# Fifteen of the twenty weight-row sums in each feed-forward chunk issued on GpSimd in place of VectorE

## The chip, the cores and the metric

The kernel runs on one core of one Trainium2 chip. The metric is the device time of one execution in microseconds (us). The kernel before takes 1955.56 us, the median of three runs (1954.87 to 1957.17). The engines carry the names of the profile: PE (TensorE matrix products), PEld (its weight loads), DVE (VectorE), ACT (ScalarE), POOL (GpSimd) and SP (the engine that only issues DMAs here). Each engine takes its instructions strictly in program order and waits on semaphores for the others.

## The reference, cut to what matters

One layer of a hybrid model on 128 context tokens and 256 latent tokens, width 2048, everything in float32. The change lies in the last sub-layer:

```python
h = rmsnorm(x, lw['norm_pre_ffn']) * (1.0 + sc2) + sh2
ff = (jax.nn.silu(h @ lw['w_ffn_gate']) * (h @ lw['w_ffn_up'])) @ lw['w_ffn_down']
x = x + ga2 * rmsnorm(ff, lw['norm_post_ffn'])
```

The hidden width is 5632, and the 384 tokens are three blocks of 128.

## The kernel before, in words

**Split numbers.** Every matrix product is made with each float32 operand split in two parts: `hi`, the operand rounded to the matrix engine's format, and `lo`, the rest. A product is then three products (hi by hi, hi by lo, lo by hi). For each weight block of 128 partitions by 1024 elements (512 KB) ACT makes `whi` by a copy with rounding (line 1430), and DVE makes `wlo`, the block less `whi` (line 1441). Both stand in rings of four tiles.

**Chunks.** The hidden width is cut into 11 chunks of 512 columns. Chunk 0 is made in the plain way. For chunks 1 to 10 the kernel saves products by a scheme in the manner of Strassen's: it replaces some weight blocks by sums and differences of blocks. For the gate and up weights, with g0, g1, u0, u1 the upper and lower row halves of the chunk's gate and up blocks (each in four pieces, i = 0 to 3), the steps are

- A: products with u0; then u0's tile becomes g0 - u0 (`sum1`, line 1413, four sums)
- B: products with g0 - u0
- C: products with g1; the tile of g0 - u0 becomes g1 - g0 + u0 (`x`, line 1437, four sums) and g0's tile becomes g1 - g0 (`y`, line 1438, four sums)
- E: products with g1 - g0 + u0, which the C just ahead of it made
- F: products with g1 - g0
- G: products with u1; the tile of E becomes u1 less what stood there (line 1440, four sums)
- H: products with that last sum

A part of the down weights goes the same way in steps DA to DH, one piece each: one sum at DA (line 1443), two at DC (lines 1437 and 1438), one at DG (line 1440). That makes 12 + 8 = 20 sums in a chunk: 4 + 4 + 4 + 4 for gate and up, 1 + 1 + 1 + 1 for down. The down steps of a chunk run inside the following chunk, so chunks 1 to 9 hold 20 sums each, and chunk 10 only the 16 of gate and up. (Written out: 40 + 9 at each of lines 1437, 1438 and 1440, 40 at line 1413 and 9 at line 1443, 196 in all.) The order of the steps is written out by hand in `steps`: A, B, then C and E in turn, F and G in turn, then H, with the down steps in between.

**Where the blocks live.** Pieces of kinds A and B (and DA, DB) are loaded into resident slots `u` and `dw`, which the sums overwrite. Pieces of kinds C, G, D, DC and DG stream through a ring of two tiles named `raw`. A `raw` tile may be loaded anew only when all its readers are done: the ACT copy, the DVE rest, and the sums that read it.

**The order of work around a step.** Each step calls `grab2`: it takes the oldest finished pair (`whi`, `wlo`), lets SP issue loads into free tiles (`load_more`), and prepares a coming block (`split_next`): first the ACT copy, then up to three or four small waiting pieces of work from the list `pend`, then the sums of that block, then the rest `wlo`. The engines' own order is therefore the order of this text (a manual schedule). The list `pend` also holds `to_sums` (line 1634): ACT copies a product bank to an SBUF tile (line 1638) and POOL issues a DMA that adds it to a sum in DRAM (line 1642). Sixteen such DMAs are issued in a chunk from the second on, 128 in all, and before the change they are POOL's only work in chunks 1 to 10.

**Memory of the operands.** The sums and the rests read two operands that both lie in SBUF. The tiles `ptr`, `pgu`, `pdn`, `z`, `zx`, `prow` and `py` lie in PSUM, so a DVE instruction that reads one of them has at most one operand in SBUF. Before the change POOL makes elementwise sums at three places only: lines 1181 and 225 just ahead of the feed-forward sub-layer, and line 1856 at the very end.

Of the kernel before, what the change touches and what calls it, by code (L numbers as in the profile page):

```python
# [96 lines left out]
def tile_step(ctx: ExitStack, tc: tile.TileContext, a, o):  # L97
    nc = tc.nc
    PE, ACT, DVE, POOL, SP = nc.tensor, nc.scalar, nc.vector, nc.gpsimd, nc.sync
# [512 lines left out]
    with ExitStack() as s:  # L612
# [203 lines left out]
        for c in range(2):  # L816

            dst = a2.rearrange("p (h d j) -> p d h j", d=2, j=P)[:, c]
            raw, up = (x.rearrange("p (h j) -> p h j", j=P) for x in (raw3[1 + c][0:98, 0:512], part[0:98]))
# [28 lines left out]
    with ExitStack() as s:  # L848
# [166 lines left out]
        for b, i in mix_order:  # L1015
# [9 lines left out]
            else:  # L1025
# [4 lines left out]
                g, y = gates.pop((b, i))  # L1030
# [14 lines left out]
    with ExitStack() as s:  # L1045
# [294 lines left out]
        for c in range(1, NFC):  # L1340
# [7 lines left out]
            for kinds in ("A", "B", "CE", "FG", "H"):  # L1348
                for i in range(4):
                    for k in kinds:  # L1350
                        steps.append((k, c, i))
                        x = after.get((k, i))
# [34 lines left out]
        def slot(x, kind, c, i):  # L1387

            return 8 + x if kind[0] == "D" else 4 * ((c + x) % 2) + i
# [20 lines left out]

        def sum1(c, i):
            x, y = (slots[slot(n, "A", c, i)] for n in range(2))
            DVE.tensor_sub(x, y, x)

        def settle_pend(n=3):
            for _ in range(n):
                if pend:
                    pend.pop(0)()

        def split_next():  # L1420

            if not entries:
                settle_pend()
                return
            kind, c, i, raw = entries.pop(0)
            x, y = (slots[slot(n, kind, c, i)] if kind not in "RD" else None for n in range(2))
            k = kind[-1]
            src = raw if kind == "R" or kind in STREAM else y if k == "F" else x
            hi, lo = (wp.tile([P, G], F32R, tag=t, name=t, bufs=4) for t in ("whi", "wlo"))
            ACT.copy(hi, src)  # L1430
            settle_pend(4 if kind in "AB" else 3)
            if (kind, i) == ("A", 3):
                sum1(c, 0)
            elif kind == "B" and i < 3:
                sum1(c, i + 1)
            elif k == "C":
                DVE.tensor_sub(x, raw, x)
                DVE.tensor_sub(y, raw, y)
            elif k == "G":
                DVE.tensor_sub(x, raw, x)  # L1440
            DVE.tensor_sub(lo, src, hi.bitcast(F32))  # L1441
            if kind == "DA":
                DVE.tensor_sub(x, y, x)
            if raw is not None:
                out_now[0] -= 1
            elif k == "F":
                free.add(slot(1, kind, c, i))
            elif k == "H":
                free.add(slot(0, kind, c, i))
            ready.append((hi, lo))  # L1450

        def grab2(kept=2):
            w = take()
            while now:
                now.pop(0)()
            load_more(kept)
            split_next()
            return w
# [487 lines left out]
```

## Time and profile before

| what | value |
| --- | --- |
| median of the runs | 1955.56 us |
| the profiled execution's own time | 1956.43 us |
| its span in the trace | 1954.6 us |
| what lies around the span | 1.83 us |
| granted TensorE clock, share of full | 0.999 |
| chunks 1 to 10, from the first PE product of step A of chunk 1 on | about 968 to 1888 us of the span |
| period of a chunk in the middle (two chunks from 1270.02 to 1456.12 us) | 93.05 us |

Rows of groups read: line, engine, operation, output and inputs by the program's names, shape, count, then busy us and mean ns of one, then the engine's idle time just before them with what ended it. Rows of windows read: start and end, length, then busy us and instruction count of each engine, the granted clock, the DMA engines' busy share and GB/s.

### The profile page before, as it was taken

The page shows a single profiled execution, that of the slowest core. Times are in us where ns is not written, and L with a number is a line of the kernel's source. Part 1 is how long each engine was busy: PE and PEld are TensorE (multiplying, and loading weights), DVE is VectorE, ACT ScalarE, POOL GpSimd, SP SyncE. Part 2 cuts the span into 40 slices and gives each one's busy share as a digit, 9 for nine tenths or more (in the row PEclk, how much of TensorE's full clock was granted, in tenths as well). Part 3 has the DMA queues.
Part 4 walks back from the last instruction along what each step waited for, and adds up shares of the span by engine and source line. Part 5 has one row for each costly group of instructions (what it writes and reads, how often), then busy time and mean ns, then how long its engine had stood idle before and what let it go on. Part 6 is the DMA issues. An engine that isn't in the chain of part 4 may idle for free.

```text
span 1954.6 us, 28091 instructions
## 1 busy us (share of the span) xinstructions
PE 1935.7 (99%) x10522; PEld 1715.2 (88%) x10522; DVE 1639.9 (84%) x2047; ACT 1011.9 (52%) x1468; POOL 144.4 (7%) x172
## 2 busy tenths in 40 slices
PE   8999999999999999999999999999999999999998
PEld 6779999999999999999988888888888888888876
DVE  5569788878876797977799989999999999988975
ACT  4233454454335655446456555555556565656444
POOL 0000000000000000004000111111112021111001
PEclk9999999999999999999999999999999999999999
DMA  9977677767764687655447686786869595949463
GB/s 389 374 259 266 222 251 238 226 220 258 249 200 155 218 269 242 215 173 201 144 145 245 160 237 171 217 206 194 222 182 234 169 239 158 264 117 254 134 212 108
DMA packets 212456, 422.05 MB, mean 216 GB/s; under 512 B 16732, under 2 KB 115228, under 8 KB 207968
## 3 DMA queue, kind: packets, MB, share of 16 engines
q1 hardware_dynamic: 193744, 386.31, 58.8%
q0 software_dynamic: 18432, 33.56, 11.1%
q8 instruction: 82, 1.34, 0.3%
q14 instruction: 54, 0.44, 0.1%
q10 hardware_dynamic: 144, 0.39, 0.1%
HBM read 365.68 MB, written 54.53 MB: 215 GB/s over the span
## 4 chain that ended last, share of the span: by engine, by line
PE 94%; DMA 2%; DVE 2%; ACT 1%; issue 0%; SPq 0%; POOL 0%; DVEq 0%; ACTq 0%; POOLq 0%
PE pmm L258 35%; PE pgu L1532 30%; PE pdn L1532 10%; PE pds L1532 7%; PE pv L398 3%; PE pgm L381 1%; DMA slab<-in_w_ada 1%; PE pf L996 1%; PE px L416 1%; PE pmm L1251 1%; PE ptr L1596 1%; DMA raw<-in_w_d 1%; DVE wlo L1441 1%; PE po L645 1%; PE pf L997 0%
## 5 line engine op out<-in xcount | busy, mean ns | idle before, releaser
L258 PE MATMUL pmm<-A_hi,whi 128*128 128x384 f32 x1200 | 404.5, 337 | 0.0
L258 PE MATMUL pmm<-A_hi,wlo 128*128 128x384 f32 x1200 | 401.6, 335 | 0.0
L258 PE MATMUL pmm<-A_lo,whi 128*128 128x384 f32 x1200 | 401.5, 335 | 0.0
L1430 ACT CAST whi<-u 128x1024 fp32r<-128x1024 f32 x200 | 209.5, 1052 | 154.2 <-PE pgu L1532 49.9
L224 ACT CAST whi<-raw 128x1024 fp32r<-128x1024 f32 x181 | 190.0, 1052 | 187.7 <-DMA raw<-in_w_gate 65.7
L225 DVE TENSOR_TENSOR wlo<-raw,whi 128x1024 fp32r<-128x1024 f32 x179 | 218.4, 1222 | 57.0 <-ACT whi L224 56.2
L1430 ACT CAST whi<-raw 128x1024 fp32r<-128x1024 f32 x157 | 165.4, 1053 | 185.0 <-DMA raw<-in_w_d 49.4
L1441 DVE TENSOR_TENSOR wlo<-u,whi 128x1024 fp32r<-128x1024 f32 x200 | 242.6, 1220 | 17.3 <-ACT whi L1430 16.6
L1532 PE MATMUL pgu<-whi,A_hi 128*128 128x512 f32 x640 | 252.5, 394 | 1.4 <-ACT ep L1573 0.9
L1532 PE MATMUL pgu<-whi,A_lo 128*128 128x512 f32 x640 | 249.6, 390 | 0.0
L258 PEld LDWEIGHTS pmm<-A_hi,whi 128*128 128x128 f32 x1200 | 225.4, 188 | 2.9 <-issue 1.8
L258 PEld LDWEIGHTS pmm<-A_lo,whi 128*128 128x128 f32 x1200 | 225.4, 188 | 0.2
L258 PEld LDWEIGHTS pmm<-A_hi,wlo 128*128 128x128 f32 x1200 | 225.3, 188 | 0.0
L572 DVE SCALAR_TENSOR_TENSOR adacc<-adaw,spad,adacc 128x1024 f32<-128x1024 f32 x180 | 222.9, 1280 | 2.5 <-DMA adaw<-in_w_ada 2.3
L1441 DVE TENSOR_TENSOR wlo<-raw,whi 128x1024 fp32r<-128x1024 f32 x157 | 191.6, 1220 | 15.3 <-ACT whi L1430 12.9
L1532 PE MATMUL pgu<-wlo,A_hi 128*128 128x512 f32 x640 | 186.0, 390 | 0.0
L1532 PEld LDWEIGHTS pgu<-whi,A_hi 128*128 128x128 f32 x640 | 120.2, 188 | 28.9 <-ACT whi L1430 2.0
L1532 PEld LDWEIGHTS pgu<-wlo,A_hi 128*128 128x128 f32 x640 | 120.2, 188 | 25.5
L1532 PEld LDWEIGHTS pgu<-whi,A_lo 128*128 128x128 f32 x640 | 120.3, 188 | 24.2
L1532 PE MATMUL pgu<-whi,S 128*128 128x512 f32 x400 | 117.6, 392 | 0.0
L1642 POOL DMA_DIRECT2D sums_d<-dw x64 | 58.4, 948 | 642.5 <-ACT dw L1638 637.2
L1532 PE MATMUL pdn<-whi,hid_hi 128*128 128x512 f32 x264 | 102.8, 390 | 0.0
(401 smaller groups left out, 3273.0 us busy)
## 6 DMA issues: line engine op xcount, KB each, us to landing
adaw<-in_w_ada SPq DMA_DIRECT2D x96, 512.0 KB, 4.3
raw<-in_w_d SPq DMA_DIRECT2D x70, 512.0 KB, 3.7
slab<-in_w_ada SPq DMA_DIRECT2D x32, 1024.0 KB
raw<-in_w_gate SPq DMA_DIRECT2D x64, 512.0 KB, 4.5
raw<-in_w_g SPq DMA_DIRECT2D x48, 512.0 KB, 4.7
raw<-in_w_u SPq DMA_DIRECT2D x48, 512.0 KB, 6.3
raw<-in_w_in SPq DMA_DIRECT2D x44, 512.0 KB, 4.5
u<-in_w_u SPq DMA_DIRECT2D x40, 512.0 KB, 7.6
```

The costliest lines, as they stand in the source:

```text
L224: ACT.copy(hi, raw)
L225: sub = lambda: eng.tensor_sub(lo, raw, hi.bitcast(F32))
L258: PE.matmul(dst, w[wi][:, k * n + n0 : k * n + n0 + P], x[xi][:, k0 + k, :], start=first and k == 0 and j == 0, stop=last and k == kts - 1 ...
L381: PE.matmul(pgv[q : q + 32, :], spad[:, k, :], slab[k // (KT // 2)][:, k % (KT // 2), :], start=k < 4, stop=k >= KT - 4,)
L398: PE.matmul(pv[2 * t + g], hT[x_][:, kb, t * P : (t + 1) * P], w_[:, g * 512 : (g + 1) * 512], start=kb == 0 and j == 0, stop=kb == KT - 1 ...
L416: PE.matmul(px, w_[:, u * P : (u + 1) * P], hT[x_][:, kb, :], start=j == 0, stop=j == 2)
L572: DVE.scalar_tensor_tensor(acc[:, c, :], w, spad[:, k, c : c + 1], acc[:, c, :], op0=ALU.mult, op1=ALU.add,)
L645: PE.matmul(dst, w[wi], x[xi], start=first and j == 0, stop=last and j == 2)
L1430: ACT.copy(hi, src)
L1441: DVE.tensor_sub(lo, src, hi.bitcast(F32))
L1532: PE.matmul(dst, stat[x_][m], mov(w[w_], m), start=first and w_ == m == x_ == 0, stop=last and w_ == m == 1, skip_group_check=any(more),)
L1642: POOL.dma_start(sums_d[k], u, accum_op=ALU.add)
```

## The change

`sum1` and the sums at lines 1438, 1440 and 1443 are issued on POOL instead of DVE. The sums at line 1437 (the `x` of C and DC, whose result the next step E or DE reads) stay on DVE. Operands, tiles and results are the same, and so are the instructions of PE and ACT and their order.

```diff
         def sum1(c, i):
             x, y = (slots[slot(n, "A", c, i)] for n in range(2))
-            DVE.tensor_sub(x, y, x)
+            POOL.tensor_sub(x, y, x)
...
             elif k == "C":
                 DVE.tensor_sub(x, raw, x)
-                DVE.tensor_sub(y, raw, y)
+                POOL.tensor_sub(y, raw, y)
             elif k == "G":
-                DVE.tensor_sub(x, raw, x)
+                POOL.tensor_sub(x, raw, x)
             DVE.tensor_sub(lo, src, hi.bitcast(F32))
             if kind == "DA":
-                DVE.tensor_sub(x, y, x)
+                POOL.tensor_sub(x, y, x)
```

Of the 196 sums 147 move: twelve in each of ten chunks and three more in each of nine; 49 stay.

On DVE, at a step C of a middle chunk (`u_9221` and `u_9222` are tiles that hold the resident slots, `raw` a streamed piece):

```order
 L1441 TENSOR_TENSOR wlo<-u_9222,whi 128x1024
 L1437 TENSOR_TENSOR u_9221<-raw,u_9221 128x1024
-L1438 TENSOR_TENSOR u_9222<-raw,u_9222 128x1024
 L1441 TENSOR_TENSOR wlo<-raw,whi 128x1024
 L1441 TENSOR_TENSOR wlo<-u_9221,whi 128x1024
```

The second of the two sums of a streamed piece is gone from DVE; the first, and the rests of this block and of the next (step E), close up.

On DVE, at steps F and G with the down steps between them (`u012`, `u345` and `u67` are the tiles of the resident slots, `dw` holds a piece of the down weights, `acc5` is the accumulator of a modulation vector that is made on the side):

```order
 L1474 SCALAR_TENSOR_TENSOR acc5_9747<-w5_9748,spad_68,acc5_9747 128x512 x2
-L1440 TENSOR_TENSOR u345_9222<-raw_9938,u345_9222 128x1024
 L1441 TENSOR_TENSOR wlo_10012<-raw_9938,whi_10011 128x1024
 L1441 TENSOR_TENSOR wlo_10031<-dw_9638,whi_10030 128x1024
 L1441 TENSOR_TENSOR wlo_10042<-u012_9221,whi_10041 128x1024
-L1440 TENSOR_TENSOR u67_9223<-raw_9972,u67_9223 128x1024
 L1441 TENSOR_TENSOR wlo_10055<-raw_9972,whi_10054 128x1024
```

No sum is left on DVE in this stretch; what remains are the rests, each with both operands in SBUF.

On POOL, where the same stretch of the program held nothing but the DMA issues of line 1642, now stands, from the four sums of steps A and B to those of the down steps ahead of G:

```order
L1413 TENSOR_TENSOR u_9222<-u_9221,u_9222 128x1024 x2
L1413 TENSOR_TENSOR u_9223<-u_9221,u_9223 128x1024
L1413 TENSOR_TENSOR u_9223<-u_9222,u_9223 128x1024
L1438 TENSOR_TENSOR u_9221<-raw,u_9221 128x1024 x2
L1443 TENSOR_TENSOR dw<-dw 128x1024
L1642 DMA sums_d<-dw 128x512 x2
L1642 DMA sums_d<-spare 128x512
L1438 TENSOR_TENSOR u_9221<-raw,u_9221 128x1024
L1642 DMA sums_d<-spare 128x512
L1642 DMA sums_d<-dw 128x512
L1438 TENSOR_TENSOR u_9222<-raw,u_9222 128x1024
L1438 TENSOR_TENSOR dw<-raw,dw 128x1024
```

The sums stand between the DMA issues, in one queue with them: a sum that follows an issue cannot start before ACT has made the copy for which that issue waits.

## The prediction, made before the changed kernel was run

> **What bounds the kernel now.** I read the page first, then PE's waits and the windows of the stage that the change touches, and last the instructions of DVE and POOL one by one.
>
> ```profile
> span 1954.6 us, 28091 instructions
> PE 1935.7 (99%) x10522; PEld 1715.2 (88%) x10522; DVE 1639.9 (84%) x2047; ACT 1011.9 (52%) x1468; POOL 144.4 (7%) x172
> ```
>
> POOL is nearly idle and DVE is loaded to 84%, which is what invites the change; but PE is at 99%. The next two views ask whether DVE ever holds PE up in chunks 1 to 10. The first lists PE's waits from 960 to 1905 us, the second each engine's busy time in stretches.
>
> ```profile
> engine line waited for: us in total, times, longest us
> PE pdn L1532 <- DVE hidE L1598: 1.4, 1, 1.4
> PE pgu L1532 <- ACT ep L1573: 0.9, 1, 0.9
> PE pgu L1532 <- ACT whi L1430: 0.4, 1, 0.4
> ```
>
> ```profile
> core 0: us, PE busy (x) PEld busy (x) DVE busy (x) ACT busy (x) POOL busy (x), PEclk, DMA share, GB/s
> 968.00:1888.00 920.00, 918.61 (x4150) 757.23 (x4149) 847.17 (x879) 529.93 (x648) 112.21 (x128) 1.00 0.71 193
> 1270.02:1456.12 186.10, 186.10 (x847) 153.72 (x846) 174.30 (x184) 109.19 (x136) 28.04 (x32) 1.00 0.77 204
> 1359.50:1411.50 52.00, 52.00 (x231) 43.06 (x230) 50.03 (x51) 29.15 (x36) 7.88 (x9) 1.00 0.74 182
> 1411.50:1452.00 40.50, 40.50 (x186) 33.53 (x185) 36.51 (x41) 25.23 (x32) 6.15 (x7) 1.00 0.81 234
> 1800.00:1893.00 93.00, 93.00 (x418) 76.98 (x417) 77.39 (x79) 44.61 (x50) 2.65 (x3) 1.00 0.55 164
> ```
>
> In 920 us PE stands still for 920 - 918.61 = 1.39 us, at a granted clock of 1.00. PE is the bound, and the whole prize for a faster DVE is 1.4 us. But DVE comes close behind: 174.30 of 186.10 us in two chunks, that is 87.2 of 93.05 in each. Within a chunk it is uneven. In the 52 us from 1359.5 (steps C to G, nearly all streamed blocks) DVE is idle for 2.0 us; in the 40.5 us after it (G to B) for 4.0. So the change cannot gain, and can lose as soon as it takes more DVE time in the dense stretch than it gives back.
>
> **The change, part by part.**
>
> What DVE gives up:
>
> ```profile
> L1440 DVE TENSOR_TENSOR u<-raw,u 128x1024 f32<-128x1024 f32 x40 | 48.8, 1221 | 20.5 <-DMA raw<-in_w_u 20.5
> L1438 DVE TENSOR_TENSOR u<-raw,u 128x1024 f32<-128x1024 f32 x40 | 48.8, 1219 | 0.0
> L1413 DVE TENSOR_TENSOR u<-u,u 128x1024 f32<-128x1024 f32 x40 | 48.7, 1218 | 0.0
> L1443 DVE TENSOR_TENSOR dw<-dw 128x1024 f32<-128x1024 f32 x9 | 11.0, 1225 | 0.3
> L1440 DVE TENSOR_TENSOR dw<-raw,dw 128x1024 f32<-128x1024 f32 x9 | 11.0, 1220 | 2.4 <-DMA raw<-in_w_d 2.4
> L1438 DVE TENSOR_TENSOR dw<-raw,dw 128x1024 f32<-128x1024 f32 x9 | 11.0, 1218 | 0.0
> ```
>
> That is 3 x 40 + 3 x 9 = 147 sums. One lasts 1.22 us, but in a row they start closer together:
>
> ```profile
> 1377.28 1.22 DVE L1437 TENSOR_TENSOR u<-raw,u 128x1024 f32<-128x1024 f32 x1
> 1378.42 1.22 DVE L1438 TENSOR_TENSOR u<-raw,u 128x1024 f32<-128x1024 f32 x1
> 1379.56 1.22 DVE L1441 TENSOR_TENSOR wlo<-raw,whi 128x1024 fp32r<-128x1024 f32 x1
> ```
>
> So each frees 1.14 us: 17.1 us in a chunk with fifteen.
>
> What POOL takes on. The nearest row is the same operation and shape on POOL, ahead of this sub-layer:
>
> ```profile
> L225 POOL TENSOR_TENSOR wlo<-raw,whi 128x1024 fp32r<-128x1024 f32 x2 | 4.8, 2412 | 0.0
> L1642 POOL DMA_DIRECT2D sums_d<-dw x64 | 58.4, 948 | 642.5 <-ACT dw L1638 637.2 <-ACT whi L1430 5.3
> L1642 POOL DMA_DIRECT2D sums_d<-spare x64 | 64.0, 1164 | 130.6 <-ACT spare L1638 130.6
> ```
>
> Fifteen at 2.41 us are 36 us, beside 28.04 / 2 = 14 us of DMA issues: 50 of 93 us. POOL itself does not become the bound.
>
> What it does to DVE is the open cost, and the trace shows it only in part:
>
> ```profile
> 916.46 0.55 DVE L1177 TENSOR_TENSOR t<-Blo,prow 128x384 f32<-128x384 f32 x1
> 916.48 2.41 POOL L225 TENSOR_TENSOR wlo<-raw,whi 128x1024 fp32r<-128x1024 f32 x1
> 916.92 0.56 DVE L1215 TENSOR_TENSOR z<-Clo,prow 128x384 f32<-128x384 f32 x1
> 917.48 0.56 DVE L1233 TENSOR_TENSOR A_lo<-z,A_hi 128x384 fp32r<-128x384 f32 x1
> 917.95 0.54 DVE L1177 TENSOR_TENSOR t<-Blo,prow 128x384 f32<-128x384 f32 x1
> 918.84 3.00 POOL L1181 TENSOR_TENSOR Clo<-t,Clo 128x384 f32<-128x384 f32 x3
> ```
>
> DVE runs on here at 0.54 to 0.56 us, undisturbed. But each of these DVE instructions has one operand in PSUM (`prow`, `z`) and one in SBUF; no row of this trace has a DVE instruction with two SBUF operands beside a POOL sum, and these are what DVE does in chunks 1 to 10. The bounds for what one POOL sum takes from DVE are therefore 0 (as in these rows) and 2.36 us, its whole time (918.84 less 916.48). Which end? POOL's sum takes twice DVE's 1.22 us, as if it fetched its two operands in turn over one path, where DVE fetches both at once. If POOL's one path is the second of DVE's, a DVE instruction with one SBUF operand goes free, as seen, and one with two waits. I take that reading, and so the upper end, because it fits both the doubled time and the free rows; the zero end needs a third path of which no row speaks.
>
> The Trainium skill ("SBUF — State Buffer", section "Who interferes with whom") states this outright: a DVE instruction with two SBUF inputs contends with a GpSimd instruction that reads SBUF, whoever starts first holds the shared interface for the whole instruction, and the other is fully blocked. The undisturbed rows agree with its other half, that one SBUF input does not contend; the blocking itself no run here shows. By that rule the sum is the one below, by the rows alone it could also be nothing.
>
> The sum, by stretch. In the dense stretch ten of the fifteen moved sums fall (the rows of 1359.5 to 1411.5 us: four at line 1438 and three at line 1440 on `u`, three on `dw`). Not every POOL sum meets a DVE instruction with two SBUF operands:
>
> ```profile
> L1472 DVE TENSOR_SCALAR acc<-w,spad 128x512 f32<-128x512 f32 x2 | 0.9, 484 | 0.0
> L1598 DVE TENSOR_TENSOR hid_lo<-ptr,hid_hi 128x512 fp32r<-128x512 f32 x1 | 0.7, 685 | 0.0
> L1580 DVE TENSOR_TENSOR ep<-ep,pgu 128x512 f32<-128x512 f32 x1 | 0.7, 680 | 0.0
> ```
>
> These 2.3 us and the idle 2.0 us are 8% of the stretch. DVE's demand becomes 50.03 - 10 x 1.14 + 10 x 2.36 x 0.92 = 60.3 us, and I leave it 1.5 of the 2.0 us that it idles waiting for ACT and for loads: 61.8 us, or **+9.8 us** on 52. In the rest of the chunk five sums move: 36.51 - 5.7 + 11.8 = 42.6 us of demand at most, against 40.5. There more of DVE's work has an operand in PSUM:
>
> ```profile
> L1598 DVE TENSOR_TENSOR hid_lo<-ptr,hid_hi 128x512 fp32r<-128x512 f32 x2 | 1.4, 688 | 0.5 <-ACT hid_hi L1598 0.5
> L1607 DVE TENSOR_TENSOR dw<-dw,ptr 128x256 f32<-128x256 f32 x2 | 0.8, 419 | 0.0
> L1608 DVE TENSOR_TENSOR dw<-ptr,dw 128x256 f32<-128x256 f32 x2 | 0.8, 420 | 0.0
> L1589 DVE TENSOR_TENSOR ep<-ep,pgu 128x512 f32<-128x512 f32 x1 | 0.7, 685 | 0.0
> L1582 DVE TENSOR_TENSOR ep<-ep,pgu 128x512 f32<-128x512 f32 x1 | 0.7, 683 | 0.0
> L1585 DVE TENSOR_TENSOR ep<-ep,pgu 128x512 f32<-128x512 f32 x1 | 0.7, 683 | 0.0
> L1586 DVE TENSOR_TENSOR ep<-ep,pgu 128x512 f32<-128x512 f32 x1 | 0.7, 682 | 0.0
> ```
>
> With its 5.8 us and 4.0 us of idle a quarter of the stretch is free of meetings, so **+0 to 2, say +0.7**. A stretch in which PE is the bound cannot make good what the dense one lost. That is 10.5 us a chunk, 94.5 us in nine chunks. The last chunk has twelve moved sums and more room: 77.39 - 13.7 + 28.3 = 92.0 of 93 us; +2. The four-deep rings of `whi` and `wlo` are a stock to be used up once, no more. Sum: +97 us on the profiled execution's 1956.43, which lies 0.9 above the median of the runs; **2053 us**.
>
> What is late then: DVE's rest `wlo`, then PE, which waits for it; ACT's copies behind, since rings come free later; and the loads into `raw`. PE's order and ACT's are unchanged and cost nothing of themselves.
>
> The queue on POOL: a sum may stand behind a DMA issue that waits for an ACT copy (the 637 us in the row above are such waits). It matters for lines 1438 and 1440, which hold a `raw` tile until they are done. From below it costs nothing: on DVE the tile was free three instructions after landing, 3.4 us; on POOL and DVE side by side 2.4 us. From above, two issues (about 2.1 us) ahead of each of the ten streamed sums, 21 us a chunk. I take nothing, as the stock of four pairs lies between, and keep the rest for the upper end.
>
> **The rivals.**
>
> *No contention at all.* Place: DVE's rests beside POOL's sums. They run at 1.22 us each, DVE falls to about 70 of 93 us, and PE, which stood still for 1.39 us, sets the time as before: 1955.5 us, at best 1954. It decides as long as a POOL sum takes less from DVE than it frees and the idle share, 1.14 + 2.0 / 10 = 1.34 us in the dense stretch. For it speak the undisturbed rows at 916 to 919 us; against it, that all of them have an operand in PSUM. This is the case that ends on the other side: not slower.
>
> *POOL waits, DVE does not.* The two exclude each other, but DVE, back to back, keeps the path, and POOL's sums slip into gaps and into the less loaded stretch. Then only the total counts: in a chunk DVE's instructions with two SBUF operands (87.2 - 17.1, less 2.3 + 5.8 with at most one) are 62.0, with POOL's 15 x 2.36 = 35.4 they fill 97.4 us for 93.05: +4.4 in each of nine chunks, 1996 us. Against it: F's operand comes from line 1438 and H's from line 1440, so the sums cannot slip far.
>
> *The queue alone.* No blocking, but `raw` tiles held longer behind the DMA issues, at a third of the upper price above less what a lighter DVE makes good, 3 us a chunk (an estimate): 1983 us.
>
> *A gain* of over 0.2% would need 3.9 us from a PE that idles 1.4.
>
> **How the numbers follow.** Blocking of DVE, my forecast: 0.72, with its own range 2015 to 2121: the low end has a sum block for 1.85 us, midway between the threshold of 1.34 and 2.36 (38.6 + 18.5 + 1.5 = 58.6 us in the dense stretch, +6.6 in nine chunks); the high end has all 35.4 us blocked and DVE's 5.9 idle us of a chunk kept (87.2 - 17.1 + 35.4 + 5.9 = 111.4 us, +18.4 in nine chunks). POOL waits: 0.08. The queue alone: 0.06. No contention: 0.13. A gain: 0.01. A measurement of this kernel can tell about 0.2% from no change, so faster 0.01, same 0.13, slower 0.86. The range must leave out no more than 2 in 10: it lets go of "no contention", the gain and a few hundredths above, and holds all the rest, 1975 to 2125.
>
> **What would show it.** DVE's rests at line 1441 longer than 1.22 us, or idle time before them with no releaser, just where POOL's sums lie; DVE's instructions with a PSUM operand still at 0.68 us; new PE waits on `wlo` of line 1441, in steps C to G above all; chunks of some 103 us for 93; POOL's sums at 2.4 us or more. I am wrong if the rests beside POOL's sums stay at 1.22 us and the chunk at 93 us, or if PE's new waits end on ACT's copies after POOL's sums (then lateness of POOL, not blocking of DVE, is the cause).

## The result and the profile after

The changed kernel takes 2092.27 us (median of four runs, 2089.84 to 2095.29) against 1955.21 us before: a ratio of 1.07, 95% interval 1.0681 to 1.0718. The forecast was slower, 2053 us with a range of 1975 to 2125: the direction and the mechanism held, the size was some 40 us short. The times below are from the profiled executions.

The page of the changed kernel:

```profile
span 2090.7 us, 28265 instructions
PE 1980.8 (95%) x10522; PEld 1732.3 (83%) x10522; DVE 1789.3 (86%) x1900; ACT 1008.6 (48%) x1468; POOL 565.5 (27%) x319
```

DVE executes 147 instructions fewer than before (1900 for 2047) and is busy for 149 us longer (1789.3 for 1639.9). That is the finding in one line: work was taken away from the engine, and its busy time rose. PE's waits in the changed kernel, from 960 to 2030 us, show whom it waits for now:

```profile
engine line waited for: us in total, times, longest us
PE pgu L1532 <- DVE wlo L1441: 39.5, 20, 4.6
PE pgu L1532 <- ACT ep L1573: 28.9, 9, 4.8
PE pds L1532 <- DVE wlo L1441: 20.6, 13, 4.1
```

Before, all of PE's waits in chunks 1 to 10 came to 1.4 us; now 60 us are waits for DVE's rests and 29 us for an ACT copy (followed back under the experiments). The groups of DVE in the same window:

```profile
L1441 DVE TENSOR_TENSOR wlo<-u,whi 128x1024 fp32r<-128x1024 f32 x200 | 348.2, 1752 | 24.3 <-ACT whi L1430 15.3 <-PE pdn L1532 8.0 <-DMA u<-in_w_g 0.5
L1474 DVE SCALAR_TENSOR_TENSOR acc<-w,spad,acc 128x512 f32<-128x512 f32 x120 | 131.0, 1131 | 0.0
L1441 DVE TENSOR_TENSOR wlo<-dw,whi 128x1024 fp32r<-128x1024 f32 x45 | 102.5, 2278 | 0.9 <-ACT whi L1430 0.6
L1437 DVE TENSOR_TENSOR u<-raw,u 128x1024 f32<-128x1024 f32 x40 | 71.9, 1798 | 1.9 <-DMA raw<-in_w_g 1.5
L1598 DVE TENSOR_TENSOR hid_lo<-ptr,hid_hi 128x512 fp32r<-128x512 f32 x27 | 18.3, 678 | 0.0
L1580 DVE TENSOR_TENSOR ep<-ep,pgu 128x512 f32<-128x512 f32 x10 | 6.7, 674 | 0.0
```

The first four read two SBUF operands, and their mean rose: the rests from 1.22 us to 1.75 and 2.28, the sums of line 1437 from 1.22 to 1.80, the accumulations of line 1474 from 0.75 to 1.13. The last two read one operand from PSUM and stayed at 0.68 and 0.67 us. The means mix two kinds, which the trace shows one by one: of the 386 rests, 236 have no POOL sum beside them and last 1.21 to 1.23 us as before, and 150 have one and last 2.74 us on average. Of the instructions of lines 1580, 1589 and 1598, 26 lie beside a POOL sum, and they last 0.67 to 0.68 us. A blocked instruction shows here as a longer instruction, not as idle time before it, so the idle column stays small. The records of POOL's sums became longer too:

```profile
L1440 POOL TENSOR_TENSOR u<-raw,u 128x1024 f32<-128x1024 f32 x40 | 130.4, 3260 | 47.8 <-DMA raw<-in_w_u 44.6 <-DVE psums L1680 3.0
L1413 POOL TENSOR_TENSOR u<-u,u 128x1024 f32<-128x1024 f32 x40 | 114.2, 3258 | 70.7 <-DVE wlo L1441 56.2 <-issue 13.2 <-DMA psums<-sums_d 1.2
```

3.26 us for the 2.41 of the prediction's row. The records overlap (line 1413's forty are busy for 114.2 us together, 2.86 each), so their length overstates what POOL lost.

Now the stage and one chunk by windows. Changed kernel, chunks 1 to 10, then the dense stretch (steps C to G) and the rest of the chunk in its middle:

```profile
core 0: us, PE busy (x) PEld busy (x) DVE busy (x) ACT busy (x) POOL busy (x), PEclk, DMA share, GB/s
968.00:2024.00 1056.00, 964.08 (x4157) 775.70 (x4156) 996.39 (x732) 526.27 (x648) 528.19 (x273) 0.96 0.63 169
1417.20:1481.50 64.30, 57.51 (x241) 46.37 (x240) 61.42 (x41) 29.74 (x37) 36.37 (x20) 0.95 0.65 165
1481.50:1525.30 43.80, 41.31 (x187) 33.58 (x186) 42.41 (x36) 25.05 (x32) 21.38 (x12) 1.00 0.69 191
```

The same two stretches of a chunk in the kernel before, cut at the same instructions:

```profile
1359.50:1412.50 53.00, 53.00 (x235) 43.91 (x234) 51.03 (x51) 29.15 (x36) 8.67 (x10) 1.00 0.75 186
1412.50:1452.10 39.60, 39.60 (x182) 32.76 (x181) 35.61 (x41) 25.33 (x32) 5.37 (x7) 1.00 0.80 229
```

The dense stretch grew by 11.3 us and the looser one by 4.2. In these two stretches DVE is now busy for 96 and 97% of the time, and PE for 89 and 94%. DVE's books for the stage: busy 847.17 us before, less 147 x 1.14 = 168 freed, and 996.39 now; so 317 us were added by blocking, **2.16 us for each POOL sum**, nearly twice what moving it frees. (The kernel below in which no engine makes the 147 sums gives the freed time directly: DVE is busy for 689.89 us there, so 157 us are freed and 306 added, 2.09 us a sum.) PE's books for the same 136 us: it waits for 92 us (1056 - 964.08) where it waited for 1.4, and it is busy for 45 us longer (964.08 for 918.61), with a clock of 0.96 in place of 1.00.

A place where this can be watched, in steps F and G of a middle chunk. POOL makes two sums of line 1440 with a DMA issue between:

```profile
1463.77 3.06 POOL L1440 TENSOR_TENSOR u<-raw,u 128x1024 f32<-128x1024 f32 x1
1466.42 1.24 POOL L1642 DMA_DIRECT2D sums_d<-dw  x1
1467.03 3.01 POOL L1440 TENSOR_TENSOR u<-raw,u 128x1024 f32<-128x1024 f32 x1
```

On DVE two accumulations take 7.22 us where they took 1.41 (the first is held for 6.55 us, through both sums), and the rest that PE needs stands behind them:

```profile
1464.04 7.22 DVE L1474 SCALAR_TENSOR_TENSOR acc<-w,spad,acc 128x512 f32<-128x512 f32 x2
1471.18 1.21 DVE L1441 TENSOR_TENSOR wlo<-raw,whi 128x1024 fp32r<-128x1024 f32 x1
```

PE finishes its products with `whi`, waits for that `wlo`, and goes on at half its pace (four products in 2.08 us; before, four took 1.07):

```profile
1467.75 0.39 PE L1532 MATMUL pgu<-whi,A_lo 128*128 128x512 f32 x1
1472.45 2.08 PE L1532 MATMUL pgu<-wlo,A_hi 128*128 128x512 f32 x4 [4.32 <-DVE wlo L1441]
```

### The profile page after: what moved, and what is told of

The parts are those of the page before. It is cut to its first block, busy times and chain, and to the rows that moved or that the text cites. A ratio compares the mean times of both kernels' runs of the same rounds, so it can differ in the third digit from the quotient of the medians.

```text
span 2090.7 us, 28265 instructions
## 1 busy us (share of the span) xinstructions
PE 1980.8 (95%) x10522; PEld 1732.3 (83%) x10522; DVE 1789.3 (86%) x1900; ACT 1008.6 (48%) x1468; POOL 565.5 (27%) x319
## 3 DMA queue, kind: packets, MB, share of 16 engines
q8 instruction: 82, 1.34, 0.3%
## 4 chain that ended last, share of the span: by engine, by line
PE 69%; DVE 13%; issue 9%; DMA 5%; ACT 2%; POOL 1%; SPq 0%; DVEq 0%; ACTq 0%; POOLq 0%
PE pmm L258 33%; PE pgu L1532 14%; DVE wlo L1441 8%; PE pdn L1532 8%; PE pds L1532 4%; PE pv L398 3%; DMA raw<-in_w_u 2%; PE pgm L381 1%; ACT whi L1430 1%; DMA slab<-in_w_ada 1%; DMA raw<-in_w_d 1%; PE pf L996 1%; DVE acc L1474 1%; PE px L416 1%; PE pmm L1251 1%
## 5 line engine op out<-in xcount | busy, mean ns | idle before, releaser
L1441 DVE TENSOR_TENSOR wlo<-u,whi 128x1024 fp32r<-128x1024 f32 x200 | 348.2, 1752 | 24.3 <-ACT whi L1430 15.3
L1441 DVE TENSOR_TENSOR wlo<-raw,whi 128x1024 fp32r<-128x1024 f32 x157 | 264.3, 1684 | 38.5 <-ACT whi L1430 35.1
L1532 PE MATMUL pgu<-whi,A_hi 128*128 128x512 f32 x640 | 257.7, 403 | 30.2 <-ACT ep L1573 28.9
L225 DVE TENSOR_TENSOR wlo<-raw,whi 128x1024 fp32r<-128x1024 f32 x179 | 217.9, 1220 | 52.7 <-ACT whi L224 52.0
L1532 PE MATMUL pgu<-wlo,A_hi 128*128 128x512 f32 x640 | 195.9, 406 | 39.7 <-DVE wlo L1441 39.5
L1438 POOL TENSOR_TENSOR u<-raw,u 128x1024 f32<-128x1024 f32 x40 | 126.3, 3159 | 157.1 <-DMA raw<-in_w_g 157.1
L1440 POOL TENSOR_TENSOR u<-raw,u 128x1024 f32<-128x1024 f32 x40 | 130.4, 3260 | 47.8 <-DMA raw<-in_w_u 44.6
L1413 POOL TENSOR_TENSOR u<-u,u 128x1024 f32<-128x1024 f32 x40 | 114.2, 3258 | 70.7 <-DVE wlo L1441 56.2
```

The costliest lines, as they stand in the source:

```text
L225: sub = lambda: eng.tensor_sub(lo, raw, hi.bitcast(F32))
L1413: POOL.tensor_sub(x, y, x)
L1438: POOL.tensor_sub(y, raw, y)
L1440: POOL.tensor_sub(x, raw, x)
L1532: PE.matmul(dst, stat[x_][m], mov(w[w_], m), start=first and w_ == m == x_ == 0, stop=last and w_ == m == 1, skip_group_check=any(more),)
```

## Experiments

**The price of a meeting, measured by itself.** A stretch is added behind the end of the kernel before, on tiles of its own:

```diff
+        phase()
+        both()
+        phase()
+        pool()
+        phase()
+        pool()
+        both(12)
+        phase()
+        pool()
+        for k in range(18):
+            DVE.tensor_sub(W[k % 2][:, 0:512], ps, ra[:, 0:512])
+        phase()
+        for k in range(16):
+            POOL.memset(L[k % 2].bitcast(F32), 0.5)
+        both(12)
+        phase()
+        pool()
+        for k in range(16):
+            DVE.tensor_scalar_mul(W[3].bitcast(F32), ra, 0.5)
...
```

Here `both(n)` makes n DVE subtractions of 128x1024 with two SBUF operands (six where no number stands), `pool()` makes four such subtractions on POOL, and `phase()` is an ACT copy for which both engines wait, so that they start together. `ps` lies in PSUM. The bursts of PE products at the end of the stretch are left out above.

> The kernel before with a stretch added behind its end (its outputs are the reference's; the time is longer by the stretch and says nothing). In the stretch DVE and POOL run alone and beside each other on tiles of their own, and PE runs bursts of 40 products between waits of growing length. Contention over operands in SBUF: DVE's 128x1024 subtractions with two SBUF operands, 1.22 us alone, stretch beside POOL's 128x1024 subtractions so that one POOL instruction costs DVE about 2.2 us, and POOL's own grow from 2.41 to 3 or more; DVE's 128x512 subtractions with one operand in PSUM stay at 0.68 us beside the same POOL work; DVE's subtractions stay at 1.22 us beside POOL memsets, which read nothing. No contention (the rests in the changed kernel grew for another reason): all stay at their times alone. Clock: if PE runs at half rate for some time after a wait, the products after the longer waits start about 0.43 us apart in place of 0.227 for some 3.4 us, those after short waits (below about 2 us) do not.

DVE in the added stretch, in this order: alone, beside POOL's subtractions, with a PSUM operand beside them, beside memsets, and scaling beside subtractions:

```profile
1966.16 6.90 DVE L1886 TENSOR_TENSOR prw<-pra 128x1024 fp32r<-128x1024 f32 x6 [15.81 <-ACT pra L1882]
1984.67 22.29 DVE L1886 TENSOR_TENSOR prw<-pra 128x1024 fp32r<-128x1024 f32 x12 [11.61 <-ACT pra L1882]
2008.15 10.86 DVE L1902 TENSOR_TENSOR prw<-prp,pra 128x512 fp32r<-128x512 f32 x18 [1.19 <-ACT pra L1882]
2020.20 13.71 DVE L1886 TENSOR_TENSOR prw<-pra 128x1024 fp32r<-128x1024 f32 x12 [1.19 <-ACT pra L1882]
2035.08 19.68 DVE L1910 TENSOR_SCALAR prw<-pra 128x1024 f32<-128x1024 f32 x16 [1.17 <-ACT pra L1882]
```

POOL in the same stretch, alone first:

```profile
1974.33 9.23 POOL L1890 TENSOR_TENSOR prl<-pra 128x1024 fp32r<-128x1024 f32 x4 [24.66 <-ACT pra L1882]
1984.72 13.22 POOL L1890 TENSOR_TENSOR prl<-pra 128x1024 fp32r<-128x1024 f32 x4 [1.15 <-ACT pra L1882]
2008.19 9.27 POOL L1890 TENSOR_TENSOR prl<-pra 128x1024 fp32r<-128x1024 f32 x4 [10.26 <-ACT pra L1882]
```

Six alone take 6.90 us, which is 1.14 apart, so twelve take 13.7 alone, as they do beside memsets. Beside four POOL subtractions they take 22.29: 8.6 us more, 2.15 for each POOL subtraction, close to the 2.09 to 2.16 of the changed kernel. POOL's four grow from 9.23 to 13.22 us, 1.0 each, about one DVE instruction's time: in this stretch the two engines take turns, an instruction at a time. With a PSUM operand neither is slowed (DVE's eighteen start 0.60 us apart, as the like do in the kernel before, and POOL's four take 9.27). This shows the contention and its price apart from everything else in the kernel. The Trainium skill ("SBUF — State Buffer", section "Who interferes with whom") has the same three cases: a DVE instruction with two SBUF inputs contends with a GpSimd instruction that reads SBUF, not with one that only writes it, and a DVE instruction with at most one SBUF input does not contend as long as it is outside the 2-port perf modes. These rows agree with each of them.

The turns do not carry over to the changed kernel. In eight of its ten chunks a single rest is held through three sums of line 1413 that POOL makes in a row, 8.3 to 9.2 us for one instruction. Why POOL gets the next turn there and not in the added stretch stays open.

**The work taken away, and the work without its reads.** First the 147 sums are made by no engine (shown against the changed kernel):

```diff
         def sum1(c, i):
             x, y = (slots[slot(n, "A", c, i)] for n in range(2))
-            POOL.tensor_sub(x, y, x)
+            return
...
-                POOL.tensor_sub(y, raw, y)
-            elif k == "G":
-                POOL.tensor_sub(x, raw, x)
...
-            if kind == "DA":
-                POOL.tensor_sub(x, y, x)
```

> The 147 moved sums are left out, on either engine (the later products use the tiles as they were). PE bounds the kernel before: 1951 to 1957 us, although DVE does 168 us less. If a lighter DVE were worth something by itself: below 1950 us.

Measured: 1954.24 us against 1957.08, ratio 0.9987 (0.9977 to 0.9996). DVE, busy for 157 us less, is worth 2.8 us (0.8 to 4.5 by the interval), of which 1.4 are the PE waits of before: PE is now busy for all of the 920 us from 968 to 1888. Then POOL gets a substitute at the same places that writes but does not read (the other three places likewise):

```diff
-                POOL.tensor_sub(y, raw, y)
+                for _ in range(2):
+                    POOL.memset(y, 0.25)
...
```

> In place of each moved sum POOL fills the same tile by two memsets (0.96 us each), at the same place of its queue and behind the same DMA issues; the sums themselves are left out. Contention for operands read from SBUF: POOL reads nothing, so DVE's rests stay at 1.22 us and the time is 1953 to 1965 us. Lateness of POOL's queue (ACT waits for tiles that POOL writes late): most of the loss stays, above 2030 us.

Measured: 1953.77 us, ratio 0.9987 (0.9978 to 0.9997). DVE's rests in that kernel, and POOL's fills at the place of line 1440's sums:

```profile
L1444 DVE TENSOR_TENSOR wlo<-u,whi 128x1024 fp32r<-128x1024 f32 x200 | 243.0, 1222 | 94.6 <-ACT whi L1431 85.2 <-PE pdn L1536 8.0 <-DMA sums_d<-dw 0.5
```

```profile
L1443 POOL MEMSET u<- 128x1024 f32 x80 | 89.9, 1125 | 24.0 <-DVE wlo L1444 21.6
```

POOL is at work at the same places of its queue, and ACT reads what it writes; the loss is gone and the rests are at 1.22 us. ACT's waits for the tiles that line 1413 writes tell how late they come: 21.1 us in all in the kernel before, where DVE writes them, 21.7 with the fills and 32.9 in the changed kernel. Two fills (1.9 us) are somewhat shorter than a sum and do not hold a `raw` tile, so this alone does not clear the queue of all blame. On the `raw` tiles the traces say this much: ACT's waits for loads into them are 85 us in the kernel before and 96 in the changed one, for a loss of 136.

**The sums ahead of the DMA issues.**

```diff
+            if (kind, i) == ("A", 3):
+                sum1(c, 0)
+            elif kind == "B" and i < 3:
+                sum1(c, i + 1)
+            elif k == "C":
+                POOL.tensor_sub(y, raw, y)
+            elif k == "G":
+                POOL.tensor_sub(x, raw, x)
             settle_pend(4 if kind in "AB" else 3)
-            if (kind, i) == ("A", 3):
...
-                POOL.tensor_sub(y, raw, y)
-            elif k == "G":
-                POOL.tensor_sub(x, raw, x)
+            if k == "C":
+                DVE.tensor_sub(x, raw, x)
```

> The changed kernel with the sums of C, G and sum1 written ahead of the pending pieces of their step, so that POOL makes them before the DMA issues of the same step. Contention: the sums block DVE as before, 2080 to 2100 us. Lateness of the queue: the sums no longer wait for those ACT copies, below 2040 us.

Measured: 2093.21 us, ratio 1.0705 (1.0687 to 1.0722), the changed kernel's loss in full. Being late behind a DMA issue of the same step is not what costs. The issues of earlier steps still stand ahead of the sums in this kernel, so the run says nothing of those.

**The length of a sum, and the threshold.** POOL makes each moved sum over a part of its columns only (at all four places; one is shown):

```diff
-                POOL.tensor_sub(y, raw, y)
+                POOL.tensor_sub(y[:, 0:512], raw[:, 0:512], y[:, 0:512])
...
```

> POOL makes each moved sum over 512 of its 1024 columns; the other half is left out. From the rows of POOL (1.02 us for 384 columns, 2.41 for 1024) such a sum takes about 1.26 us. The threshold of the prediction (1.34 us taken from DVE by a sum) says that the dense stretch then needs 38.6 + 10 x 1.26 x 0.92 + 1.5 = 51.7 of 52 us: 1953 to 1970 us. If the loss came from the places of the sums in POOL's queue and not from their length: above 2040 us. If it came in proportion to the length, without a threshold: about 2024 us.

> The same over 768 columns (a quarter left out), about 1.81 us a sum: 38.6 + 10 x 1.81 x 0.92 + 1.5 = 56.8 us in the dense stretch, +4.8 us in nine chunks, 43 us of new PE waits, and half as much again if PE runs slower after waits as in the changed kernel: 2000 to 2025 us. In proportion to the length without a threshold: about 2058 us.

Measured with 512 columns: 1965.94 us, ratio 1.0055 (1.0035 to 1.0075). With 768: 2021.73 us, ratio 1.0328 (1.0312 to 1.0343). With all 1024: 1.07. The loss, against 1956.18 us for the first two and 1955.21 for the last, is 10, 66 and 137 us: it starts near half the length and then rises steeply, as it must if DVE first uses up its reserve and only then holds PE up. A loss in proportion to the length (68 and 103 us) is excluded, and so is one that comes from the sums' places alone. By the books above a half sum takes 0.9 to 1.0 us from DVE and a three-quarter sum 1.6 (DVE is busy for 826.47 and 918.71 us over the stage).

**Which sums carry it.** Only the 40 of line 1413 on POOL, and then all the others:

```diff
 (the kernel before)
-            DVE.tensor_sub(x, y, x)
+            POOL.tensor_sub(x, y, x)
 (the changed kernel)
-            POOL.tensor_sub(x, y, x)
+            DVE.tensor_sub(x, y, x)
```

> Only the 40 sums of line 1413 go to POOL, all others stay on DVE. By the prediction's sum for the looser stretch: +0 to 2 us a chunk, 1955 to 1980 us. If a late sum at the chunk's start is what matters (PE's waits for ACT at line 1573 in the changed kernel, 29 us): 1990 us or more.

> The other 107 sums go to POOL, line 1413 stays on DVE. By the prediction's sum the dense stretch carries nearly the whole loss: 2050 to 2090 us. If each sum cost the same wherever it stands (137 us / 147): about 2055 us together with 1992 us for the kernel with the 40 alone; if the sums at the chunk's start carried it: below 2020 us.

Measured: 1982.87 us with the 40 alone, ratio 1.0137 (1.012 to 1.0155), and 2047.31 us with the 107, ratio 1.0472 (1.0447 to 1.0497). The 107 cost 91 us, just below the expected 2050 to 2090 us; the 40 at the chunk's start cost 27 us, above the expected 1955 to 1980 us, and less than the 34 or more that the rival put on them. So the dense stretch carries most of the loss, but not nearly all of it: that is 0.85 us a sum for the 107 and 0.67 for the 40, not far from equal shares, and together the two parts cost 137 us, not 118. PE's waits with the 40 alone say through whom:

```profile
PE pgu L1532 <- ACT ep L1573: 17.7, 8, 2.7
```

In the changed kernel the same spot reads so, on POOL, then on DVE, then on PE:

```profile
1502.89 0.87 POOL L1642 DMA_DIRECT2D sums_d<-dw  x1 [10.14 <-ACT dw L1638]
1503.43 2.11 POOL L1642 DMA_DIRECT2D sums_d<-spare  x2
1504.53 8.14 POOL L1413 TENSOR_TENSOR u<-u,u 128x1024 f32<-128x1024 f32 x3
```

```profile
1504.55 10.35 DVE L1441 TENSOR_TENSOR wlo<-u,whi 128x1024 fp32r<-128x1024 f32 x2 [0.49 <-ACT whi L1430]
1514.82 0.68 DVE L1598 TENSOR_TENSOR hid_lo<-ptr,hid_hi 128x512 fp32r<-128x512 f32 x1
```

```profile
1519.78 0.50 PE L1532 MATMUL pgu<-whi,A_hi 128*128 128x512 f32 x1 [2.02 <-ACT ep L1573]
```

Three sums stand behind three DMA issues, the first of which waited 10.14 us for an ACT copy; then POOL makes the sums in one go, where DVE in the kernel before made the like with starts 2.3 and 3.5 us apart. Two rests on DVE take 10.35 us where they took 2.3, and the first of them alone 9.22 us, through all three sums. `hid_lo` comes late, ACT waits for it in its order (52.8 us over the stage, at line 1606, for 6.7 before), and the copy of the product banks (line 1573) for which PE waits stands behind. Looseness on average does not help against a cluster. How much of the cluster is POOL's queue was not tried: in the kernel with the sums written ahead, the same three issues still precede the same three sums.

**One operand, and the clock.** A second added stretch:

```diff
+        phase()
+        for k in range(16):
+            DVE.tensor_scalar_mul(W[3].bitcast(F32), ra, 0.5)
+        phase()
+        for k in range(8):
+            POOL.tensor_copy(L[k % 2].bitcast(F32), ra)
+        phase()
+        for k in range(8):
+            POOL.tensor_copy(L[k % 2].bitcast(F32), ra)
+        both(12)
...
+        for n in (0, 1, 2, 3, 4, 5, 6, 8):
+            DVE.tensor_sub(W[0][:, 512:640], ps[:, 0:P], ra[:, 0:P])
+            for k in range(n):
+                DVE.tensor_sub(W[0][:, 512:640], W[0][:, 512:640].bitcast(F32), ra[:, 0:P])
+            burst(48, W[0])
```

Here `burst(n, src)` makes n PE products of 128x512.

> The kernel before with another stretch added behind its end (outputs are the reference's, the time is longer by the stretch). DVE's 128x1024 scaling with one SBUF operand alone, for the 16 that took 19.68 us beside four POOL subtractions in the first probe: about 10.5 us if POOL blocked it too, 19 us if not. POOL copies, which read one SBUF operand, beside twelve DVE subtractions with two: DVE's twelve grow from 13.71 us by about a copy's whole time for each copy if any reading by POOL blocks, and stay at 13.7 us if only two-operand POOL work does. Clock: PE bursts after waits that grow in small steps from about 0.8 to 2.5 us; if a wait of some 2 us is the threshold (the changed kernel shows no slowing after 2.0 us and slowing after 2.25), the first bursts run at 0.227 us a product throughout and the last ones have some 3.4 us at half rate.

DVE's scaling alone, and its twelve subtractions beside POOL's copies:

```profile
1970.94 11.62 DVE L1894 TENSOR_SCALAR prw<-pra 128x1024 f32<-128x1024 f32 x16 [16.67 <-ACT pra L1882]
1992.84 20.43 DVE L1886 TENSOR_TENSOR prw<-pra 128x1024 fp32r<-128x1024 f32 x12 [10.29 <-ACT pra L1882]
```

POOL's copies, alone and beside them:

```profile
1983.82 7.92 POOL L1897 COPY prl<-pra 128x1024 f32<-128x1024 f32 x8 [30.24 <-issue]
1992.87 15.92 POOL L1900 COPY prl<-pra 128x1024 f32<-128x1024 f32 x8 [1.14 <-ACT pra L1882]
```

Eight copies cost DVE 20.43 - 13.71 = 6.7 us, 0.84 each, for a copy of 0.99 us: a POOL instruction that reads a single SBUF operand blocks too, for most of its length. And the scaling, with its single SBUF operand, took 19.68 us beside four POOL subtractions and takes 11.62 alone: 2.0 us for each, blocked like the rest. PE's bursts of 48 products after waits of growing length:

```profile
2082.38 11.20 PE L1907 MATMUL prp<-prw 128*128 128x512 f32 x48 [1.69 <-DVE prw L1914]
2095.58 12.84 PE L1907 MATMUL prp<-prw 128*128 128x512 f32 x48 [2.01 <-DVE prw L1914]
2126.38 12.80 PE L1907 MATMUL prp<-prw 128*128 128x512 f32 x48 [3.00 <-DVE prw L1914]
```

After waits up to 1.69 us a burst takes 11.2 us; after 2.01, 2.34 and 3.00 us it takes 1.4 to 1.6 us more. (The bursts of the first added stretch came after waits of 2.04 us and longer, and every one of them ran in part at half clock.) In the changed kernel the granted clock around the wait of 4.32 us shown above:

```profile
1468.00:1472.00 4.00, 0.14 (x1) 0.00 (x0) 4.00 (x3) 0.00 (x0) 2.04 (x1) 0.87 0.80 198
1472.00:1476.00 4.00, 3.55 (x8) 2.82 (x9) 4.00 (x5) 0.00 (x0) 0.00 (x0) 0.50 0.65 231
1476.00:1480.00 4.00, 4.00 (x15) 3.20 (x14) 3.31 (x3) 2.48 (x3) 3.12 (x2) 0.78 1.07 369
```

It falls to 0.50. Over the stage the trace has the clock at half for 75 us in 14 pieces, and PE is busy for 62 of these, which accounts for about 31 of PE's 45 us of longer busy time.

## Why the prediction was right, and where it fell short

*PE bounds the kernel, and a lighter DVE is worth nothing.* Right, nearly: with the sums on no engine the kernel gains 2.8 us. The prize was put at 1.4.

*DVE instructions with two SBUF operands are blocked by a POOL sum, those with a PSUM operand are not.* Right, shown by the rows of DVE in the changed kernel, by the first probe, and by the memsets in place of the sums. The prediction took 2.36 us for a meeting and let 92% of the sums meet in the dense stretch, 2.17 us; measured are 2.15 in the added stretch and 2.09 to 2.16 in the kernel. That the product fits so well is in part luck: a meeting costs 2.15 us, less than taken, and nearly every sum meets, more than taken. Its wording, that an instruction with one SBUF operand goes free, was too wide: a scaling from SBUF to SBUF is blocked as well. Only the PSUM operand of the quoted rows was shown free, and the rule that the prediction cites has a condition (outside the 2-port perf modes) that its wording leaves out; whether the scaling runs in such a mode no run here shows.

*The dense stretch: +9.8 us.* It became +11.3. DVE's demand of 60.3 us was right: it is 61.42 in a stretch cut one microsecond longer, 60.4 like for like. The miss is idle time, 2.9 us and not 1.5.

*The looser stretch: +0 to 2, taken as 0.7 us.* This is the term that was mis-sized. It became +4.2. The prediction had written down DVE's demand without any free meetings, 42.6 us, and then let a quarter of the sums fall into idle time and beside instructions with a PSUM operand. Measured is 42.41 us in 43.8, in a stretch cut 0.9 us shorter: that relief did not come. The sums of line 1413 run in a cluster beside DVE's rests, and POOL, which is not bound to DVE's order, works on six sums in this stretch and not five (the last of line 1440 at 1481.29 us and the first of line 1438 for the next step C at 1517.11 us lie in it too). In the middle chunk this term is 3.5 us short and the dense one 1.5. The nine periods from chunk 1 to chunk 10 (from the first copy of line 1573 in one to that in the next) grew by 130 us together, where 94.5 was forecast: by 8.9 and 9.7 us the first and the last of them, by 14.3 to 17.6 the others. That is 36 of the 39 us missing (136 of span for 97). From there to the end of the span another 4.6 us were lost, where +2 was forecast for the last chunk.

*POOL's queue costs nothing.* Right for the issues of a sum's own step: written ahead of them, the sums cost the same. For the cluster at the chunk's start, which stands behind the issues of an earlier step, it stays open. The prediction named a sign of lateness, new PE waits that end on ACT's copies, and 29 of PE's 92 us do end there; followed back, ACT was waiting for `hid_lo`, which stood on DVE behind a held rest.

*The rivals.* "No contention" and "the queue alone" fell with the probe, the memsets and the sums ahead. "POOL waits, DVE does not" fell as well: in the added stretch both wait, in turns, POOL 1.0 us and DVE 2.15, and in the changed kernel a rest is held through up to three sums.

*The threshold of 1.34 us a sum.* The half sums, put at 1.26 us x 0.92 = 1.16 and measured at 0.9 to 1.0, lie below it, and 10 us are lost all the same: PE stands still for 6.4 us of the stage, 5.0 of them for ACT's copies at line 1430, which a sum over averages leaves out. The three-quarter sums (1.67 taken, 1.6 measured) land where the same arithmetic put them.

*PE's clock* was in no term. It is real, with 45 us more of PE's busy time, but it must not be added to the 317 us of DVE's books: DVE is busy for 996 of 1056 us, and where PE waits for DVE anyway, a slower PE need not make the kernel longer. How much shorter the kernel would be at full clock was not tried and stays open.

## What to carry to other kernels

Before work is moved from DVE to POOL, look where the operands of both lie. A POOL subtraction or copy that reads SBUF stopped DVE's SBUF-to-SBUF work for nearly its whole length (2.15 us for a subtraction that takes 2.31), and as POOL needs twice the time for a two-operand sum, such a move takes from DVE nearly twice what it frees; POOL work belongs beside DVE instructions with an operand in PSUM, or should only write. And read first which engine the stage waits for: here PE was full, so a lighter DVE won 0.15%, while a heavier one had only 2 us in 52 before it would show.

## What the runs showed that was not expected

A PE wait of about 2 us can be enough to halve the granted clock, for 3.4 or 6.8 us by the trace of the changed kernel. In the second added stretch 1.69 us cost only itself, and 2.01 us and longer cost 1.4 to 1.6 us more. In the changed kernel the edge is not sharp: of eight PE waits of 2.0 to 2.35 us in the stage two were followed by half clock (2.25 and 2.34 us) and six were not (among them another of 2.34); all twelve of over 3 us were. What decides between them stays open. The Trainium skill ("TensorE: Matmul & The Clock Gate", section "Part 1: The HAM clock gate (the "warmup" mystery)") gives a window of about 3.4 us of idleness before the drop; here less sufficed, and the measurement decides.

For their length, the smallest of DVE's instructions suffered most: two corrections of 128 x 8 elements at lines 1497 and 1498, 0.17 us each before, lasted 2.16 and 2.29 us on average, as a meeting costs POOL's whole length whatever DVE's own is.
